# Moving a decoder block's SBUF tiles from multiples of 64 bytes to multiples of 128

## The chip, the cores and the metric

The kernel runs on one NeuronCore of one Trainium2 chip. The metric is the device time of one execution in microseconds, the median of repeated runs. The core has five engines: TensorE (PE, whose weight loads the profile lists apart as PEld), VectorE (DVE), ScalarE (ACT), GpSimd (POOL) and SyncE (SP), which here only issues transfers. The on-chip memory SBUF has 128 partitions; a tile takes the same byte range in all of them, so "address" below means the byte offset within a partition.

## The reference

One decoder block on 512 positions of width 1024, everything in float32, cut to its steps:

```python
h = rms_norm(x, g_mix)
u, q, k, v, gate_logits = split(h @ w_in)
y_pool = causal_multiscale_pool(u, w_pool, pool_scale)      # windows 2, 4, 8, 16
q, k = apply_rope(q), apply_rope(k)
o = diff_attention(q, k, v, lam)       # 4 heads: softmax(q0 k0) - lam * softmax(q1 k1), causal, times v
y_attn = rms_norm(o, g_subln) * (1 - lam_init)
x = x + (concat([y_pool, y_attn]) * sigmoid(gate_logits)) @ w_out
x = x + memory_cross_attention(rms_norm(x, g_cross), rms_norm(mem, g_mem), w_cq, w_ckv, w_co)
x = x + square(relu(rms_norm(x, g_mlp) @ w_up)) @ w_down     # 1024 -> 4096 -> 1024
return rms_norm(x, g_final)
```

The memory `mem` has 256 rows; its product with `w_ckv` gives the keys and the values of the cross attention.

## The kernel before

Activations are kept transposed: 128 features in the partitions, 512 positions along a row. Every operand of a large product is split into a rounded part and a remainder, both float32r (`hi`, `lo`), and `mm3` (L93 to L96) adds three matmuls for each block of 128 features: hi times hi, lo of the streaming operand, lo of the weights.

```python
def mm3(o, lh, ll, rh, rl, start, stop):
    nc.tensor.matmul(o, lh, rh, start=start, stop=False)   # L94
    nc.tensor.matmul(o, lh, rl, start=False, stop=False)   # L95
    nc.tensor.matmul(o, ll, rh, start=False, stop=stop)    # L96
```

The first operand is loaded as weights (a LDWEIGHTS before each matmul), the second streams past them. `tile_mm` makes one output tile of 128x512: eight blocks, so 24 matmuls, with the weights in `whi` and `wlo` and the activations streaming.

The work runs in this order: v (L334 to L338, where `whi`/`wlo` stream and `xg` is loaded); the 20 tiles of `PLAN` (q, k, gate, u), between which a list of due steps (`after`, `tick`) puts the scores, transposes and products of the differential attention and the pooling; the output projection; the memory's keys (`mem_k`, 256 columns wide) and values (`mem_v`); the cross attention's queries with its scores in between (`cross_scores`, 256 columns), and its output; then the MLP in four groups, each of eight up tiles and eight down tiles. The last down tile is cut into two halves of 256 columns so that the final norm can begin early. Weights are fetched three tiles ahead, and VectorE and ScalarE split them two ahead. TensorE's program is in the order in which the code is written; the other engines' is set by a scheduler.

All tiles come from one pool. Each tag (`tmp`, `xg`, `whi`, ...) gets a stretch for its buffers; the stretches follow one another in the order in which the tags are first used, each buffer rounded up to 32 bytes. The first is `vx` (gains and the first block of x), 557 floats or 2228 bytes, which fills 2240. What matters of the result, with the stage in which TensorE reads it:

| tag | what it holds for TensorE | address of the first buffer before, modulo 128 | after, modulo 128 |
|---|---|---|---|
| `cst` (with `ident`) | identity for transposes | 18752, 64 | 18816, 0 |
| `tmp` | squares, pooled rows, softmax rows | 25664, 64 | 25728, 0 |
| `ones` | sums over features | 46720, 0 | 46848, 0 |
| `xg` | normed x; x1 normed; output of the cross attention; activations of the MLP | 61568, 0 | 61696, 0 |
| `whi`, `wlo` | split weights | 94336 and 106624, 0 | 94464 and 106752, 0 |
| `vr` | v | 121152, 64 | 121344, 0 |
| `s` | q, k; normed memory; queries of the cross attention | 137664, 64 | 137856, 0 |
| `at` | transposed softmax rows | 163008, 64 | 163200, 0 |
| `mix` | mixed rows; keys and values of the memory; x2 normed | 185536, 64 | 185728, 0 |

All large buffers are multiples of 1024 bytes long (`xg` and `mix` 4096, `hi` in the first half and `lo` in the second), and the slices that TensorE takes begin at multiples of 512 within them, so a tag's remainder holds for all its reads.

Of the kernel before, what the change touches and what calls it, by code (L numbers as in the profile page):

```python
# [17 lines left out]
P = 128  # L18
T = 512
# [20 lines left out]
NG_COL = LAMS  # L40
# [6 lines left out]
def block_kernel(ctx: ExitStack, tc: tile.TileContext, x0g, xT, memT, wv, wm, wckv, wpool, vecs, csts, outT):  # L47
# [14 lines left out]
    def nm(s):  # L62
        uid[0] += 1
        return f"{s}_{uid[0]}"

    def sb(tag, shape, bufs, dt=F32):
        return pool.tile(shape, dt, tag=tag, name=nm(tag), bufs=bufs)
# [10 lines left out]
    def ps(tag, bufs):  # L78
        return psum.tile([P, T], F32, tag=tag, name=nm(tag), bufs=bufs)
# [20 lines left out]
        S.copy(hi, src)  # L100
        eng.tensor_tensor(lo, src, f(hi), op=ALU.subtract)  # L101

    vx = sb("vx", [P, NG_COL + T], 1)
    vec = vx[:, :NG_COL]
    cst = sb("cst", [P, NCST], 1)
    nc.sync.dma_start(vx, x0g)
# [6 lines left out]
    warm = ps("acc", 2)  # L113
    for j in range(WARM):
        nc.tensor.matmul(warm, idle[:, :P], idle, start=j == 0, stop=j == WARM - 1)
    eps = sb("eps", [P, 16], 1)[:, :1]
    V.memset(eps, EPS)
    one_f = sb("onef", [P, P], 1)
    V.memset(one_f, 1.0)
# [46 lines left out]
    def rsqrt(dst, ssum, scale, v, l, by=None):  # L166

        V.tensor_scalar(v, ssum, scale, EPS, op0=ALU.mult, op1=ALU.add)
        S.activation(l, ssum, AF.Ln, bias=eps, scale=scale)
        S.activation(dst, l, AF.Exp, scale=-0.5)  # L170
        S.activation(l, dst, AF.Square)
        V.scalar_tensor_tensor(l, l, -0.5, v, op0=ALU.mult, op1=ALU.mult)
        if by is not None:
            by(dst)
        V.scalar_tensor_tensor(dst, l, 1.5, dst, op0=ALU.add, op1=ALU.mult)
# [18 lines left out]
    def rstd_rows(sp, n):  # L194
        hi, lo = sp
        o = ps("tr", 2)
        for i in range(n):
            c = slice(i * P, (i + 1) * P)
            nc.tensor.matmul(o[:, 2 * i:2 * i + 2], hi[:, c], ones[:, :2], start=True, stop=False)
            nc.tensor.matmul(o[:, 2 * i:2 * i + 2], lo[:, c], ones[:, :2], start=False, stop=True)  # L200
        r = sb("rrow", [P, 8], 2)[:, :2 * n]
        rsqrt(r, o[:, :2 * n], 1.0 / D, sb("rscr", [P, 8], 4)[:, :2 * n], sb("rscr", [P, 8], 4)[:, :2 * n])
        return r

# [118 lines left out]
    def v_proj():  # L323
# [18 lines left out]
        def stats():  # L342
            r = rstd_full(sp, ss)
            st["rstd"] = r
            rr = rstd_rows(sp, NT)
            V.tensor_tensor(cos_r, cos_r, r, op=ALU.mult)
            V.tensor_tensor(sin_r, sin_r, r, op=ALU.mult)
            vs = []
            for i in range(NT):
                vh = sb("vr", [P, T], 8, F32R)  # L350
                vl = sb("vr", [P, T], 8, F32R)
                scaled(vh, vl, o[i], rr[:, 2 * i:2 * i + 1])
                vs.append((vh, vl))
            st["v"] = vs
            lambdas()
# [190 lines left out]
    def mem_in():  # L546
        mg = {}
        sm = sb("ssm", [P, M], 1)
        for k2 in range(KC // 2):
            t = tmp()  # L550
            nc.sync.dma_start(t, memT[:, 2 * k2:2 * k2 + 2, :])
            pr = pair("s", 6)
            for kk in range(2):
                k = 2 * k2 + kk
                c = slice(kk * M, (kk + 1) * M)
                scaled(pr[:, 0, c], pr[:, 1, c], t[:, c], vec[:, G_MEM + k:G_MEM + k + 1])
                accumulate(sm, k, t[:, c], M)
                mg[k] = (pr[:, 0, c], pr[:, 1, c])
        st["mg"] = mg
        sp = split_sq(sm, M)  # L560

        def stats():
            st["mrstd"] = rstd_full(sp, sm, M)
            st["mrow"] = rstd_rows(sp, MT)

        after(STATM, stats)
# [273 lines left out]
```

## Time and profile before

| | |
|---|---|
| median of 3 runs | 743.44 us (742.29 to 744.35) |
| the profiled execution | 742.82 us, span 741.0 us from its first to its last instruction |
| mean granted TensorE clock | 0.994 |
| TensorE busy | 722.2 us in 3384 matmuls |
| weight loads busy | 598.8 us |
| VectorE, ScalarE, GpSimd busy | 429.4, 354.6, 58.7 us |
| DMA | 78.41 MB, mean 106 GB/s |

The busy time of an engine is that in which at least one of its instructions runs. Matmuls are pipelined: one starts before the last has ended, so their durations add up to more than the busy time, and the distance between two starts is read from the timeline, which lists the instructions by start time (us from the span's start, then the duration).

### The profile page before, as it was taken

What the parts mean: (1) busy time and instruction counts of PE and PEld (TensorE: products, weight loads), DVE (VectorE), ACT (ScalarE), POOL (GpSimd) and SP (SyncE); (2) the same over time, 40 slices, a digit from 0 to 9 for tenths busy, and PEclk for the clock granted to TensorE, in tenths of its full rate; (3) what the DMA queues carried; (4) which work ended last, traced back from release to release, by engine and by line L of the source; (5) the groups of instructions that cost most, each with busy time, mean ns of one, the idle gap of its engine ahead of it and who ended that gap; (6) DMA issues with size and microseconds to landing.
All of it is one profiled execution on the core that took longest, in us unless ns stands there. A gap on an engine that the chain in (4) does not pass through costs nothing.

```text
span 741.0 us, 8888 instructions
## 1 busy us (share of the span) xinstructions
PE 722.2 (97%) x3384; PEld 598.8 (81%) x3384; DVE 429.4 (58%) x677; ACT 354.6 (48%) x589; POOL 58.7 (8%) x50
## 2 busy tenths in 40 slices
PE   8999999999999999999999999999999999999993
PEld 5877888788889888888888888888888888888882
DVE  7597999875987546663665443453434533345336
ACT  7498998676766434343354321342214422234332
POOL 0043112534000000000000000000000000000003
PEclk9999999999999999999999999999999999999997
DMA  8433223142535541210423323223232232232203
GB/s 312 142 113 114 86 73 113 61 162 92 171 114 178 193 140 59 68 47 29 142 85 89 111 86 110 89 86 113 86 99 100 86 113 86 92 107 86 86 0 113
DMA packets 24650, 78.41 MB, mean 106 GB/s; under 512 B 2688, under 2 KB 4736, under 8 KB 24608
## 3 DMA queue, kind: packets, MB, share of 16 engines
q1 hardware_dynamic: 24560, 77.73, 32.3%
q8 instruction: 26, 0.43, 0.3%
q14 instruction: 16, 0.13, 0.1%
q0 software_dynamic: 48, 0.13, 0.0%
HBM read 73.65 MB, written 2.10 MB: 102 GB/s over the span
## 4 chain that ended last, share of the span: by engine, by line
PE 87%; DVE 5%; ACT 4%; DMA 1%; issue 1%; POOL 0%; SPq 0%; DVEq 0%; ACTq 0%
PE acc L94 25%; PE acc L96 24%; PE acc L95 24%; PE sc L94 3%; PE sc L96 3%; PE sc L95 3%; ACT tmp L395 1%; DMA tmp<-xT 1%; DVE mix L734 1%; DVE tmp L393 1%; PE sc L334 1%; ACT tmp L365 1%; PE sc L336 1%; PE sc L338 1%; ACT whi L100 1%
## 5 line engine op out<-in xcount | busy, mean ns | idle before, releaser
L100 ACT CAST whi<-wraw 128x1024 fp32r<-128x1024 f32 (+1 forms) x128 | 133.9, 1047 | 297.1 <-PE acc L95 227.5
L94 PE MATMUL acc<-xg,whi 128*128 128x512 f32 x504 | 198.6, 394 | 0.0
L96 PE MATMUL acc<-xg,wlo 128*128 128x512 f32 x504 | 196.6, 390 | 0.0
L95 PE MATMUL acc<-xg,whi 128*128 128x512 f32 x504 | 196.4, 390 | 0.0
L101 DVE TENSOR_TENSOR wlo<-wraw,whi 128x1024 fp32r<-128x1024 f32 (+1 forms) x128 | 158.3, 1237 | 33.0 <-ACT whi L100 32.6
L94 PE MATMUL acc<-mix,whi 128*128 128x512 f32 x296 | 116.3, 393 | 0.0
L96 PE MATMUL acc<-mix,wlo 128*128 128x512 f32 x296 | 116.2, 392 | 0.0
L95 PE MATMUL acc<-mix,whi 128*128 128x512 f32 x296 | 115.2, 389 | 0.0
L96 PEld LDWEIGHTS acc<-xg,wlo 128*128 128x128 f32 x504 | 94.6, 188 | 20.2
L94 PEld LDWEIGHTS acc<-xg,whi 128*128 128x128 f32 x504 | 94.7, 188 | 19.0
L95 PEld LDWEIGHTS acc<-xg,whi 128*128 128x128 f32 x504 | 94.7, 188 | 18.6
L520 DVE TENSOR_TENSOR vr<-acc,vr 128x512 f32<-128x512 f32 x41 | 28.3, 691 | 109.0 <-PE acc L96 109.0
L745 DVE SCALAR_TENSOR_TENSOR tmp<-acc,rstd 128x512 f32<-128x512 f32 x32 | 22.1, 692 | 84.4 <-PE acc L96 84.3
L96 PEld LDWEIGHTS acc<-mix,wlo 128*128 128x128 f32 x296 | 55.6, 188 | 12.6
L95 PEld LDWEIGHTS acc<-mix,whi 128*128 128x128 f32 x296 | 55.6, 188 | 12.5
L94 PEld LDWEIGHTS acc<-mix,whi 128*128 128x128 f32 x296 | 55.6, 188 | 11.4
L734 POOL TENSOR_TENSOR mix<-mix,tmp 128x256 f32<-128x256 f32 x7 | 6.2, 906 | 547.9 <-ACT mix L716 546.6
L101 DVE TENSOR_TENSOR xg<-tmp,xg 128x512 fp32r<-128x512 f32 x32 | 22.1, 692 | 0.3 <-ACT xg L100 0.3
L395 ACT ACTIVATE tmp<-tmp,small 128x128 f32<-128x128 f32 (+3 forms) x32 | 17.9, 560 | 5.8 <-DVE small L393 5.6
L100 ACT CAST xg<-tmp 128x512 fp32r<-128x512 f32 x32 | 19.8, 620 | 1.0
L746 ACT ACTIVATE tmp<-tmp 128x512 f32<-128x512 f32 x32 | 20.1, 632 | 0.0
L211 DVE TENSOR_TENSOR ss<-ss,tmp 128x512 f32<-128x512 f32 x27 | 18.6, 688 | 1.6 <-ACT tmp L210 1.4
(229 smaller groups left out, 944.9 us busy)
## 6 DMA issues: line engine op xcount, KB each, us to landing
wraw<-wm SPq DMA_DIRECT2D x108, 512.0 KB, 3.3
wraw<-wckv SPq DMA_DIRECT2D x16, 512.0 KB, 3.8
s<-s SPq DMA_DIRECT2D x8, 256.0 KB, 3.6
vr<-xT SPq DMA_DIRECT2D x8, 256.0 KB, 5.0
outT<-mix SPq DMA_DIRECT2D x8, 256.0 KB, 2.2
tmp<-xT SPq DMA_DIRECT2D x7, 256.0 KB, 6.8
wraw<-wv SPq DMA_DIRECT2D x3, 512.0 KB, 6.6
tmp<-memT SPq DMA_DIRECT2D x4, 256.0 KB, 4.7
```

Of the source, the lines that this page charges most:

```text
L94: nc.tensor.matmul(o, lh, rh, start=start, stop=False)
L95: nc.tensor.matmul(o, lh, rl, start=False, stop=False)
L96: nc.tensor.matmul(o, ll, rh, start=False, stop=stop)
L100: S.copy(hi, src)
L101: eng.tensor_tensor(lo, src, f(hi), op=ALU.subtract)
L211: V.tensor_tensor(ss, ss, sq, op=ALU.add)
L334: nc.tensor.matmul(o[i], xg[k][0][:, tb], wh[:, c], start=k == 0, stop=False)
L395: S.activation(e[:, :n], e[:, :n], AF.Exp, bias=mn, scale=-1.0, accum_out=sm[:, c:c + 1])
L520: V.tensor_tensor(t, o, t, op=ALU.add)
L734: eng.tensor_tensor(y3[j][:, i, c], y3[j][:, i, c], r, op=ALU.mult)
L745: V.scalar_tensor_tensor(t, o, 0.0, st["r2"], op0=ALU.max, op1=ALU.mult)
L746: S.activation(t, t, AF.Square)
```

## The change

Three small tiles are allocated longer, and used at their old length. `vx` becomes 576 floats (2304 bytes), `eps` goes from 64 to 128 bytes, the two buffers of `rrow` (row scales) from 32 to 64 bytes each. So the tags after them move: by 64 bytes from `cst` on, by 128 from `onef` on, by 192 from `rscr` on. Nothing else is changed: all engines run the same instructions in the same order.

```diff
-    vx = sb("vx", [P, NG_COL + T], 1)
+    vx = sb("vx", [P, NG_COL + T + 19], 1)[:, :NG_COL + T]
     vec = vx[:, :NG_COL]
...
-    eps = sb("eps", [P, 16], 1)[:, :1]
+    eps = sb("eps", [P, 32], 1)[:, :1]
...
-        r = sb("rrow", [P, 8], 2)[:, :2 * n]
+        r = sb("rrow", [P, 16], 2)[:, :2 * n]
```

## The prediction

> **What bounds the kernel now.** I read the page first (busy time, the clock row, the chain that ended last), then TensorE's waits, then its groups, and last the start times of single matmuls in the timeline.
>
> ```profile
> span 741.0 us, 8888 instructions
> ...
> PE 722.2 (97%) x3384; PEld 598.8 (81%) x3384; DVE 429.4 (58%) x677; ACT 354.6 (48%) x589; POOL 58.7 (8%) x50
> ...
> PEclk9999999999999999999999999999999999999997
> ...
> PE 87%; DVE 5%; ACT 4%; DMA 1%; issue 1%; POOL 0%; SPq 0%; DVEq 0%; ACTq 0%
> ```
>
> TensorE is busy for 97% of the span at a granted clock of 0.9 or more in every slice but the last, and it is 87% of the chain that ended last. Its list of waits begins like this and only gets shorter:
>
> ```profile
> PE sc L391 <- DMA s<-s: 1.6, 1, 1.6
> PE acc L115 <- DVE tmp L112: 1.2, 1, 1.2
> ```
>
> So what sets the time is the distance from one matmul's start to the next, and a change that issues the same instructions can gain or lose only there, or by making some operand late. The change touches addresses alone. The groups give no hint that an address matters (the last number before the second bar is the mean in ns):
>
> ```profile
> L94 PE MATMUL acc<-xg,whi 128*128 128x512 f32 x504 | 198.6, 394 | 0.0
> L94 PE MATMUL acc<-mix,whi 128*128 128x512 f32 x296 | 116.3, 393 | 0.0
> L94 PEld LDWEIGHTS acc<-xg,whi 128*128 128x128 f32 x504 | 94.7, 188 | 19.0
> L94 PEld LDWEIGHTS acc<-mix,whi 128*128 128x128 f32 x296 | 55.6, 188 | 11.4
> ```
>
> A tile `xg` that begins on a multiple of 128 bytes and a tile `mix` that begins 64 bytes past one have the same duration. But 394 ns is a pipelined matmul's length, and matmuls overlap; 3384 of them would not fit otherwise. What counts is the pitch, start to start. In a row `mix,whi` the first name is the operand that streams, the second the one that is loaded as weights. Rows of the timeline, at the borders of output tiles of the MLP (24 matmuls of 512 columns each); the first number is the start in us:
>
> ```profile
> 463.94 0.40 PE L94 MATMUL acc<-mix,whi 128*128 128x512 f32 x1
> 469.45 0.39 PE L94 MATMUL acc<-mix,whi 128*128 128x512 f32 x1
> ...
> 507.90 0.40 PE L94 MATMUL acc<-xg,whi 128*128 128x512 f32 x1
> ...
> 513.39 0.39 PE L94 MATMUL acc<-xg,whi 128*128 128x512 f32 x1
> ...
> 551.47 0.40 PE L94 MATMUL acc<-mix,whi 128*128 128x512 f32 x1
> ```
>
> Up, reading `mix`: from 469.45 to 507.90 lie seven tiles, 168 matmuls: 38.45/168 = 228.9 ns. Down, reading `xg`: 513.39 to 551.47, again 168: 38.08/168 = 226.7 ns. The first tile of each half is slower (5.51 and 5.49 us against 5.49 and 5.44). That is the one place where the trace shows a price for the 64 bytes: 2.2 ns per matmul. It is a confounded comparison, since `mix` also lies elsewhere in the memory.
>
> **The change, term by term.** The five engines' instructions and their order are the same; every tile after `vx` moves by 64 to 192 bytes. Before, `xg`, `whi`, `wlo`, `ones` lie on multiples of 128 and `cst`, `tmp`, `vr`, `s`, `at`, `mix` 64 bytes off; after, all lie on one. The pairs fall into five groups.
>
> A. `mix` streams, `whi`/`wlo` loaded. If it then runs like `xg`, a group of up matmuls takes what a down group takes: 551.47 - 507.90 = 43.57 instead of 507.90 - 463.94 = 43.96 us, 0.39 less, and there are 4 groups: 1.56 us. The output projection also streams `mix`, 8 tiles of 24; three of its tiles:
>
> ```profile
> 188.26 0.39 PE L94 MATMUL acc<-mix,whi 128*128 128x512 f32 x1
> ...
> 204.74 0.39 PE L94 MATMUL acc<-mix,whi 128*128 128x512 f32 x1
> ```
>
> 16.48/72 = 228.9 ns, the same as in the MLP, so 192 x 2.2 ns = 0.43 us. Together -2.0 us. Lower end -2.2 (all 960 at 226.7, and no slow first tile); upper end +4.2 (all at the 233.3 ns of the next term).
>
> B and C. The memory's values and keys. Keys stream `s` (64 off, 256 columns), values load `s` as weights (64 off, 512 columns streamed from `whi`):
>
> ```profile
> 216.42 0.28 PE L94 MATMUL acc<-s,whi 128*128 128x256 f32 x1
> ...
> 221.75 0.28 PE L96 MATMUL acc<-s,wlo 128*128 128x256 f32 x1
> ...
> 225.47 0.28 PE L94 MATMUL acc<-s,whi 128*128 128x256 f32 x1
> ...
> 239.60 0.40 PE L94 MATMUL sc<-whi,s 128*128 128x512 f32 x1
> ...
> 262.00 0.39 PE L94 MATMUL sc<-xg,whi 128*128 128x512 f32 x1
> ```
>
> Values: (262.00 - 239.60)/96 = 233.3 ns, the slowest pitch at 512 columns. At 226.7 they save 0.63 us; some of it may stay, as in the first tiles above, so B is -0.5 (0 to -0.6). Keys: 47 steps from 216.42 to 221.75 are 113.4 ns each (half of 226.7, nothing to gain), the 120 from 225.47 to 239.60 take 117.8. One place has 256 columns with both operands on multiples of 128, the first half of the last tile:
>
> ```profile
> 721.10 0.28 PE L94 MATMUL sc<-xg,whi 128*128 128x256 f32 x1
> ...
> 723.97 0.28 PE L94 MATMUL sc<-xg,whi 128*128 128x256 f32 x1
> ```
>
> 2.87/24 = 119.6 ns. So at 256 columns the aligned pair is slower than the misaligned. If the keys go there, 48 matmuls lose 6.2 ns and 144 lose 1.8: C is +0.6 us (from -0.6, all at 113.4, to +0.6). I take the end of the row that has the alignment the keys will have.
>
> D. Scores of the cross attention, `mix` and `s`, both 64 off, 256 columns, 4 heads of 24:
>
> ```profile
> 276.29 0.28 PE L94 MATMUL sc<-mix,s 128*128 128x256 f32 x1
> ...
> 279.16 0.40 PE L94 MATMUL acc<-xg,whi 128*128 128x512 f32 x1
> ```
>
> 2.87/24 = 119.6 ns, what the aligned pair takes too: 0 (down to -0.6 at 113.4). That equal offsets behave alike, whether 0 or 64, speaks for the relation of the two streams as the cause, and not for the line on which one begins.
>
> E. The attention phase and the small sums. Between scores, transposes and sums, q, k, gate and u tiles run in pieces of nine or so:
>
> ```profile
> 120.46 0.47 PE L94 MATMUL acc<-xg,whi 128*128 128x512 f32 x1
> ...
> 122.63 0.22 PE L390 MATMUL sc<-s,s 128*128 128x128 f32 x1
> ```
>
> 2.17 us for nine, where 226.7 ns would make 2.04. Of the 0.13 too much, 0.08 stands in the first one's length (0.47 against 0.39), which is the change of shape and stays; 0.05 is a slow pitch after the interruption. Some 30 such pieces make 1.5 us, and the interrupting matmuls themselves, about 150, are at most the 6.6 ns of term B too slow, 0.5 to 1 us. Whether an aligned interruption disturbs less is not to be seen: a down group's first tile loses the same 0.05 us (5.49 - 5.44) with aligned operands, though after a misaligned predecessor. I take -0.5 (0 to -2).
>
> The rest costs nothing by its rows. Vector work on a `vr` tile (64 off) lasts as long as on `xg` tiles:
>
> ```profile
> L520 DVE TENSOR_TENSOR vr<-acc,vr 128x512 f32<-128x512 f32 x41 | 28.3, 691 | 109.0 <-PE acc L96 109.0
> L101 DVE TENSOR_TENSOR xg<-tmp,xg 128x512 fp32r<-128x512 f32 x32 | 22.1, 692 | 0.3 <-ACT xg L100 0.3
> ```
>
> and it idled 109 us for TensorE there, so it also has cover. No transfer changes in size; the largest wait of TensorE on one is the 1.6 us above. `eps` and `rrow` are read at their first columns only, as before.
>
> Sum: -2.0 - 0.5 + 0.6 + 0 - 0.5 = -2.4 us. The profiled execution took 742.82 us (1.8 around its span) and becomes 740.4; it stands 0.6 below the median of 743.44, so against the median 741.0.
>
> **Rivals.** No change: the address does not matter, and `mix` is slow because it streams x2g and the mixed rows, or lies in another part of the memory. For it: equal durations in the groups, and every slow tile also has a high address (`s`, `mix`). Against it: `xg` is fast in the output of the cross attention and in the down half alike, so the stage is not what matters. 743.4. The Trainium skill (SBUF — State Buffer, section Specifications) gives a line of 16 bytes as the unit of full-rate access, and in its section Who interferes with whom says that TensorE never waits on anyone; both homes begin on such a line, so by it this rival holds and the sum is 0. The trace has 228.9 against 226.7 ns, which that page would have to explain otherwise.
>
> Slower: the relation between the two streams matters over a longer period than 128 bytes. Today `xg` and `whi` have the same offset modulo 256 and `mix` is 64 bytes from `whi`; afterwards `mix` is 128 bytes from `whi` modulo 256, a distance that no long run of the trace has. If those 960 matmuls then pay what the values pay, 233.3 instead of 228.9, that is +4.2, and C adds 0.6: 748.2. It decides from a pitch of about 231 ns on. The only rows near it, `at` with `vr` in the attention, are 12 matmuls that never settle.
>
> Everything settles: A, B, C and D at their low ends and E at -1.5: -2.2 - 0.6 - 0.6 - 0.6 - 1.5 = -5.5, so 737.9. For it: the keys' first 48 matmuls hold 113.4. Against it: 119.6 with both aligned.
>
> **How the numbers follow.** The sum's case 0.52, no change 0.24, everything settles 0.14, slower 0.10. A difference under 0.3% (2.2 us) is about what these runs can't tell from none. The sum's case lies just beyond it, so 0.32 of its 0.52 count as faster, with the 0.14 of full settling 0.46; 0.20 and the 0.24 of no change make 0.44 within; 0.10 slower. The range leaves out the slower case and the outer part of full settling (it ends at a gain of 4.8), and reaches 1 us above the median for no change: 738.6 to 744.4. The sum's case alone would be 739.8 to 742.2.
>
> **What would show it.** A right: 226.7 ns per matmul in the up halves, tiles of 5.44 us; wrong: still 228.9, or over 231. B: the values' 96 matmuls in 21.8 us instead of 22.4. C: 119.6 ns on all keys; at 113.4 the time comes out 1.2 us lower. E: less than 2.17 us for a piece of nine. The prediction fails at large if the up halves keep their pitch, since A is most of it, or if `xg` tiles, whose offset to `whi` stays, change theirs.

## The result: 0.6% slower

The changed kernel takes 747.72 us (median of 6 runs, 746.54 to 749.11) against 743.1 (6 runs, 742.29 to 744.35). The ratio is 1.0061, 95% interval 1.0046 to 1.0075. The forecast was 741.0, with 738.6 to 744.4 as its range.

The profiled execution took 746.97 us. Its page, in the lines that answer to those of before:

```profile
span 745.1 us, 8888 instructions
...
PE 726.2 (97%) x3384; PEld 599.4 (80%) x3384; DVE 429.7 (58%) x677; ACT 354.5 (48%) x589; POOL 58.8 (8%) x50
...
PEclk9999999999999999999999999999999999999997
...
L94 PE MATMUL acc<-xg,whi 128*128 128x512 f32 x504 | 198.6, 394 | 0.0
...
L94 PE MATMUL acc<-mix,whi 128*128 128x512 f32 x296 | 117.0, 395 | 0.0
```

The span grew by 4.1 us and TensorE's busy time by 4.0, at the same clock (0.994); the weight loads grew by 0.6, and no other engine's busy time moved by more than 0.3. Its list of waits begins with 1.5 us, as before with 1.6. So the loss is in the distance between the matmuls themselves. The groups show it only as a hint: `mix` went from 393 to 395 ns, `xg` kept its 394. The timeline at the same borders of output tiles as before (start in us first):

```profile
465.57 0.40 PE L94 MATMUL acc<-mix,whi 128*128 128x512 f32 x1
471.16 0.40 PE L94 MATMUL acc<-mix,whi 128*128 128x512 f32 x1
...
510.36 0.39 PE L94 MATMUL acc<-xg,whi 128*128 128x512 f32 x1
...
515.82 0.39 PE L94 MATMUL acc<-xg,whi 128*128 128x512 f32 x1
...
553.89 0.40 PE L94 MATMUL acc<-mix,whi 128*128 128x512 f32 x1
```

Up, on `mix`: (510.36 - 471.16)/168 = 233.3 ns per matmul, where it was 228.9. Down, on `xg`: (553.89 - 515.82)/168 = 226.6, as before. An up group takes 44.79 us instead of 43.96; four groups make +3.3. In the output projection three tiles take (205.25 - 188.45)/72 = 233.3 ns per matmul instead of 228.9, which is +0.8 on its 192:

```profile
188.45 0.40 PE L94 MATMUL acc<-mix,whi 128*128 128x512 f32 x1
...
205.25 0.40 PE L94 MATMUL acc<-mix,whi 128*128 128x512 f32 x1
```

These two are +4.1 us, the whole growth of the span. The keys and values of the memory:

```profile
217.09 0.28 PE L94 MATMUL acc<-s,whi 128*128 128x256 f32 x1
...
222.66 0.28 PE L96 MATMUL acc<-s,wlo 128*128 128x256 f32 x1
...
226.27 0.28 PE L94 MATMUL acc<-s,whi 128*128 128x256 f32 x1
...
240.52 0.39 PE L94 MATMUL sc<-whi,s 128*128 128x512 f32 x1
...
262.82 0.39 PE L94 MATMUL sc<-xg,whi 128*128 128x512 f32 x1
```

Keys: 118.5 ns in the first 47 steps (113.4 before), 14.25/120 = 118.8 after (117.8 before), +0.4 us in all. Values: 22.30/96 = 232.3 ns (233.3 before), -0.1 us. The small remainder, the other way, lies in the rest of the program.

### The profile page after: what moved, and what is told of

Same layout as the page of the kernel before. It is cut to its first block, busy times and chain, and to the rows that moved or that the text cites. A ratio compares the mean times of both kernels' runs of the same rounds, so it can differ in the third digit from the quotient of the medians.

```text
span 745.1 us, 8888 instructions
## 1 busy us (share of the span) xinstructions
PE 726.2 (97%) x3384; PEld 599.4 (80%) x3384; DVE 429.7 (58%) x677; ACT 354.5 (48%) x589; POOL 58.8 (8%) x50
## 4 chain that ended last, share of the span: by engine, by line
PE 88%; DVE 5%; ACT 4%; DMA 1%; issue 1%; POOL 0%; SPq 0%; DVEq 0%; ACTq 0%
PE acc L94 25%; PE acc L96 24%; PE acc L95 24%; PE sc L96 3%; PE sc L94 3%; PE sc L95 3%; ACT tmp L395 1%; DVE mix L734 1%; DMA tmp<-xT 1%; DVE tmp L393 1%; PE sc L334 1%; ACT tmp L365 1%; PE sc L336 1%; PE sc L338 1%; ACT whi L100 1%
## 5 line engine op out<-in xcount | busy, mean ns | idle before, releaser
L94 PE MATMUL acc<-mix,whi 128*128 128x512 f32 x296 | 117.0, 395 | 0.0
L95 PE MATMUL acc<-mix,whi 128*128 128x512 f32 x296 | 116.9, 395 | 0.0
```

## The experiments

Theory R is the prediction's slower rival: what counts is the distance between the tile that streams and the tile that is loaded as weights, modulo 256 bytes (the streaming tile's address minus the weight tile's; the two directions differ, as the table below shows). P and A are its rivals: `mix` is slow for its place far up in the memory (P), or for its own remainder (A). Times are compared with the kernel before on the same chip, 742.8 us in both sets.

**`mix` alone, one step further.** From the changed kernel, a gap ahead of `mix`:

```diff
+        if not mixed:
+            sb("gap", [P, 32], 1)
         pr = pair("mix", 8)
```

> The changed kernel, with mix alone moved on by 128 bytes, so that it lies 256 bytes from whi and wlo modulo 512 (0 modulo 256) and still on a multiple of 128. Theory R (what counts is the distance between the streaming tile and the weight tile, modulo 256): the up halves and the output projection fall from 233.3 ns per matmul to 226.7, 960 x 6.6 = 6.3 us less than the changed kernel, about 741.4. Theory P (mix is slow because it lies far up in the memory): the pitch stays at 233.3 and the time at 747.7. Theory A (what counts is the streaming tile's own remainder, 384 modulo 512 in the changed kernel): remainder 0 is one that no fast tile has had, so the pitch is open, but xg has been fast at 128 and 256. If the distance counts modulo 512, the pitch may be anything from 226.7 to 240.

It took 740.36 us, with a ratio to the kernel before of 0.997 (0.9959 to 0.9981). That is 7.4 us less than the changed kernel's median, which was timed in another set, and 6.6 by the spans of the profiled executions (738.5 against 745.1). The second to the eighth up tile lie between these rows, 38.08/168 = 226.7 ns:

```profile
468.40 0.39 PE L94 MATMUL acc<-mix,whi 128*128 128x512 f32 x1
...
506.48 0.39 PE L94 MATMUL acc<-xg,whi 128*128 128x512 f32 x1
```

`mix` is as fast as `xg` there, 128 bytes further up, so P is out. And 256 is as good as 0: what counts repeats after 256 bytes, not after 512.

**The dose: `xg` at the bad distance as well.**

```diff
+        if not ready and i == 0:
+            sb("gapw", [P, 32], 1)
         hi = sb("whi", [P, D], 3, F32R)
```

> The changed kernel with 128 bytes put between xg and whi: xg keeps its address, and whi, wlo and everything behind move on by 128. The distance of mix to whi stays 128, that of xg becomes 384 modulo 512 (128 modulo 256). Theory R: now the xg tiles pay as well, the down halves and q, k, g, u go from 226.7 to about 233.3: 1600 x 6.6 = 10.5 us more than the changed kernel, less the slow first matmuls that they have already, 756 to 758. Theories P and A: xg has not moved, so the down halves stay at 226.7 and the time at 747.7.

It took 753.33 us, ratio 1.0138 (1.0116 to 1.016): 5.6 us more than the changed kernel (6.4 by the spans, 751.5 against 745.1), less than R had named. In the down half:

```profile
519.78 0.39 PE L94 MATMUL acc<-xg,whi 128*128 128x512 f32 x1
...
558.82 0.39 PE L94 MATMUL acc<-mix,whi 128*128 128x512 f32 x1
```

39.04/168 = 232.4 ns instead of 226.6, though `xg` did not move: what streams is not slow in itself, it is slow against these weights, and A is out with it. Nor are the weights slow for their own address: in the fifth experiment below `whi` lies at 94592 as it does here, and the down halves run at 226.7 ns.

R's size was too large, for three reasons. It took 233.3 ns, and `xg` settles at 232.4 (0.9 ns less on some 1600 matmuls, 1.4 us). The 480 matmuls of q, k, g and u, whose steps average 234.1 ns with the interruptions, went only to 236.7. And `mix`, whose distance to `whi` is the same as in the changed kernel, became faster, from 233.3 to 232.4 (0.8 us on its 960), which theory R does not explain:

```profile
475.17 0.40 PE L94 MATMUL acc<-mix,whi 128*128 128x512 f32 x1
...
514.21 0.40 PE L94 MATMUL acc<-xg,whi 128*128 128x512 f32 x1
```

39.04/168 = 232.4. So one distance can settle at two pitches. The keys of the kernel before had shown the same, 113.4 ns in the first 47 steps and 117.8 later, with the same two tiles. What decides between them was not tested: the distance fixes the pitch to about 1 ns at 512 columns and to about 4 at 256.

**The part alone.** From the kernel before, `mix` on by 64 bytes: it then begins on a multiple of 128, and all tiles ahead of it lie where they did.

```diff
+        if not mixed:
+            sb("gap", [P, 16], 1)
         pr = pair("mix", 8)
```

> The kernel before with mix alone moved on by 64 bytes, so that it begins on a multiple of 128 and lies 128 bytes from whi; every tile ahead of it stays where it was. Theory R: 233.3 ns in the up halves and the output projection, 960 x 4.4 = 4.2 us more than before, 747.3 (the keys, which were the other loss of the change, do not move). The prediction's reading (a multiple of 128 is what helps): 226.7 and 741. Theory P: 743.

It took 747.77 us, ratio 1.0065 (1.0048 to 1.0081): the loss of the whole change. From 471.33 to 510.53 its seven up tiles take the 39.20 us of the changed kernel:

```profile
471.33 0.40 PE L94 MATMUL acc<-mix,whi 128*128 128x512 f32 x1
...
510.53 0.39 PE L94 MATMUL acc<-xg,whi 128*128 128x512 f32 x1
```

**The distances measured by themselves.** A kernel of nothing but matmuls, executed once, with weight tiles `wa` to `wq` 32 bytes apart modulo 512:

```python
for n in (T, M):
    for t in w:
        run(mov, t, n)              # 48 matmuls
    for k in (0, 2, 4, 6, 8, 10):
        o = run(nov, w[k], n)
```

> Leaves the block out and only runs matmuls of float32r operands: one streaming tile (mov at 128 modulo 512) against 17 weight tiles wa to wq that lie 32 bytes apart modulo 512, so that the distance falls from 384 by 32 with each letter (wm has 0, wi 128, we 256, wa 384), 48 matmuls each, first 512 columns wide and then 256; after each sweep a second streaming tile (nov at 192) against wa, wc, we, wg, wi, wk. Theory R: the pitch at 512 columns repeats every 8 letters, with 226.7 ns at wm and we, 233.3 at wi, wq and wa, 229 at wk; nov gives the same at the same distance (233.3 with wg, 226.7 with wk's neighbour in distance). Theory A: all letters are equal for mov, and differ from nov. At 256 columns R expects 120 at wm and less at a distance of 64 (wk, wc). Distances that are not multiples of 64 have not occurred yet: if the unit is 64 bytes, they go with a neighbour.

The timeline merges each 48; the pitch is the difference of two starts over 48.

```profile
52.01 11.05 PE L121 MATMUL acc<-mov,we 128*128 128x512 f32 x48
62.89 11.35 PE L121 MATMUL acc<-mov,wf 128*128 128x512 f32 x48
74.08 11.36 PE L121 MATMUL acc<-mov,wg 128*128 128x512 f32 x48
85.28 11.40 PE L121 MATMUL acc<-mov,wh 128*128 128x512 f32 x48
96.52 11.32 PE L121 MATMUL acc<-mov,wi 128*128 128x512 f32 x48
107.68 11.37 PE L121 MATMUL acc<-mov,wj 128*128 128x512 f32 x48
118.88 11.16 PE L121 MATMUL acc<-mov,wk 128*128 128x512 f32 x48
129.88 11.36 PE L121 MATMUL acc<-mov,wl 128*128 128x512 f32 x48
141.07 11.05 PE L121 MATMUL acc<-mov,wm 128*128 128x512 f32 x48
151.96 11.35 PE L121 MATMUL acc<-mov,wn 128*128 128x512 f32 x48
163.15 11.36 PE L121 MATMUL acc<-mov,wo 128*128 128x512 f32 x48
...
219.10 11.16 PE L121 MATMUL acc<-nov,we 128*128 128x512 f32 x48
230.09 11.06 PE L121 MATMUL acc<-nov,wg 128*128 128x512 f32 x48
240.99 11.36 PE L121 MATMUL acc<-nov,wi 128*128 128x512 f32 x48
252.19 11.32 PE L121 MATMUL acc<-nov,wk 128*128 128x512 f32 x48
263.35 5.86 PE L121 MATMUL acc<-mov,wa 128*128 128x256 f32 x48
```

| distance, bytes | weights, with `mov` | ns per matmul |
|---|---|---|
| 0 | `wm` | 226.9 |
| 32 | `wl` | 233.1 |
| 64 | `wk` | 229.2 |
| 96 | `wj` | 233.3 |
| 128 | `wi` | 232.5 |
| 160 | `wh` | 234.2 |
| 192 | `wg` | 233.3 |
| 224 | `wn` | 233.1 |
| 256 | `we` | 226.7 |

`nov`, 64 bytes off in itself, gives 229.0 with `we` (320, that is 64), 227.1 with `wg` (256, that is 0) and 232.5 with `wk` (128): the same by distance, another by address. The expectation's 233.3 for `nov` with `wg` was a slip: their distance is 256. So the pitch follows the distance, and of the multiples of 32 only those of 256 are fast, with 64 in second place. The direction counts: 64 gives 229.2 ns, 192 (that is -64) gives 233.3. The kernel before had `mix` at that second-best distance, 64, and the change took it to 128.

At 256 columns the order is another, and 0 is among the slowest.

```profile
303.18 5.79 PE L121 MATMUL acc<-mov,wh 128*128 128x256 f32 x48
308.81 5.85 PE L121 MATMUL acc<-mov,wi 128*128 128x256 f32 x48
314.50 5.91 PE L121 MATMUL acc<-mov,wj 128*128 128x256 f32 x48
...
331.57 5.91 PE L121 MATMUL acc<-mov,wm 128*128 128x256 f32 x48
337.31 5.84 PE L121 MATMUL acc<-mov,wn 128*128 128x256 f32 x48
```

The steps are 117.3 ns at 160, 118.5 at 128 and 119.6 at 0; at 64 they are 117.7, less than at 0, as expected. It is the 119.6 that the prediction had read from the last tile.

**Everything at distance 0.** From the kernel before, four pads that bring all of TensorE's tiles to 128 modulo 256:

```diff
-    vx = sb("vx", [P, NG_COL + T], 1)
+    vx = sb("vx", [P, NG_COL + T + 19], 1)[:, :NG_COL + T]
-    eps = sb("eps", [P, 16], 1)[:, :1]
+    eps = sb("eps", [P, 64], 1)[:, :1]
-        r = sb("rrow", [P, 8], 2)[:, :2 * n]
+        r = sb("rrow", [P, 16], 2)[:, :2 * n]
-        gsub = sb("gsub", [P, 16], 1)[:, :1]
+        gsub = sb("gsub", [P, 48], 1)[:, :1]
```

> The kernel before with pads at vx, eps, rrow and gsub, so that cst, tmp, ones, xg, whi, wlo, vr, s, at and mix all lie at 128 modulo 256, that is at distance 0 from each other modulo 256. Theory R with the table just measured (0: 226.7 ns at 512 columns, 120 at 256): mix 960 x -2.2 = -2.1 us against before, the values 96 x -6.6 = -0.6, the keys 192 x +3 = +0.6, small stages -0.3: about 740.4, no more than 0.5 us from the version that moved mix alone. A rival by which every pair has a distance of its own would leave more or less than that.

It took 739.56 us, ratio 0.9957 (0.9945 to 0.997), faster than both kernels. The values now take (260.57 - 238.78)/96 = 227.0 ns, the keys (238.78 - 224.38)/120 = 120.0:

```profile
224.38 0.28 PE L94 MATMUL acc<-s,whi 128*128 128x256 f32 x1
...
238.78 0.40 PE L94 MATMUL sc<-whi,s 128*128 128x512 f32 x1
...
260.57 0.39 PE L94 MATMUL sc<-xg,whi 128*128 128x512 f32 x1
```

**The same distances, every tile 64 bytes off.** This version has `NG_COL + T + 35` in `vx` and is otherwise the last one. No tile that TensorE reads begins on a multiple of 128.

> The last version with 64 bytes more in vx: every tile that TensorE reads now begins 64 bytes past a multiple of 128, and all distances are still 0 modulo 256. Theory R: the same time as the last version within 0.1%, about 740.4, pitch 226.7 in up and down halves. If a multiple of 128 is worth anything in itself, as the change supposes and the prediction's sum took over, it is slower: with 228.9 ns on all 2600 matmuls of 512 columns by 5.7 us.

It took 739.96 us, ratio 0.9959 (0.9947 to 0.9971): this is the last one's time, and the intervals are all but the same. A multiple of 128 is worth nothing in itself.

**Finer distances, narrower weights, bfloat16.** Again a kernel of nothing but matmuls, executed once.

> Leaves the block out and only runs matmuls, 48 of a kind, 512 columns, one weight tile wgt. First mov at distances of 0, 4, 8, 16, 32, 64, 128 and 256 bytes (banks pa to ph in this order), then weights of 64 and of 32 columns at distances 0, 64, 128 (pa, pf, pg), then bfloat16 operands at 0, 32, 64, 128, 256 bytes (pa, pe to ph), last the first pair again (pb). Theory L (the two streams of TensorE, weights and moving operand, get into each other's way while a weight load overlaps a matmul): with fewer columns of weights the penalty at 128 shrinks or goes, and 226.7 itself may fall; rival M (the penalty lies in the moving operand's own reading): it stays with 32 columns. Below 32 bytes no value is known: if a read covers 64 bytes, 4 to 16 go with 0 or with their neighbour 32 (233.3). With bfloat16 I expect near 216, as the last two of the warm-up, and a smaller effect or none, since half the bytes are read.

```profile
18.53 11.52 PE L122 MATMUL pb<-mov,wgt 128*128 128x512 f32 x48
29.89 11.35 PE L122 MATMUL pc<-mov,wgt 128*128 128x512 f32 x48
...
96.47 11.20 PE L122 MATMUL pa<-mov,wgt 128*64 128x512 f32 x48
107.51 11.16 PE L122 MATMUL pf<-mov,wgt 128*64 128x512 f32 x48
118.51 11.17 PE L122 MATMUL pg<-mov,wgt 128*64 128x512 f32 x48
129.52 11.27 PE L122 MATMUL pa<-mov,wgt 128*32 128x512 f32 x48
140.62 11.29 PE L122 MATMUL pf<-mov,wgt 128*32 128x512 f32 x48
151.75 11.23 PE L122 MATMUL pg<-mov,wgt 128*32 128x512 f32 x48
162.82 10.53 PE L122 MATMUL pa<-bmov,bwgt 128*128 128x512 bf16 x47
...
193.91 10.52 PE L122 MATMUL pg<-bmov,bwgt 128*128 128x512 bf16 x47
204.27 10.52 PE L122 MATMUL ph<-bmov,bwgt 128*128 128x512 bf16 x47
```

Four bytes are the worst distance measured, 236.7 ns; 8 and 16 give 233.1 and 231.7. With 64 columns of weights the distances 0, 64 and 128 are already nearly alike, 230.0, 229.2 and 229.4 ns, and with 32 columns they are again, 231.3, 231.9 and 230.6. That the distance stops mattering fits L, in which the overlapping weight load is one side of it; that the pitch then stays at 229 to 232, above the 226.7 that 128 columns reach at distance 0, fits neither L nor M. With bfloat16 the distances 0 to 128 give 215.8 to 216.0 ((193.91 - 162.82)/144 is 215.9 for the first three, 10.36/48 is 215.8 from `pg` to `ph`), and the steps within `ph`, at 256, are 216; one record of each 48 is missing from the trace.

That the pitch goes by the distance modulo 256, with float32r operands and 128 columns of weights, is shown, to within the 1 ns named above at 512 columns. By what mechanism the two operands hinder each other is left open.

## Why the prediction was wrong

- What bounds the kernel held: the difference is in TensorE's pitch, and none of its waits grew by more than 0.5 us.
- Term A failed, at the step "If it then runs like `xg`". It priced the 64 bytes as a property of `mix` and put -2.0 us; the runs show a property of the pair, and +4.1. Its upper end, +4.2 at the values' 233.3 ns, is where it landed. The range of the text did not take that end in, since it hung on the slower rival, which had a chance of 0.10. That rival named what counts, the place (128 modulo 256) and the time: 748.2, measured 747.72. That its time fits so well is in part luck. Its 233.3 ns came from the values, whose distance was 192, and at 128 the matmuls alone give 232.5.
- The clue was in the prediction itself. Term D noted that two tiles 64 bytes off behave like two on a multiple of 128, and that this speaks for the relation of the streams. Term A did not follow it: by relation, `xg` with `whi` is a row for distance 0, and no settled row existed for 128. The pooling's product, which streams `tmp` (64 modulo 256) past `s` (192), was a second row at 128, which the rival did not name beside `at` with `vr`: 12 matmuls in threes, 231.8 ns on average to the next start, already above the 231 from which the rival decides. An unknown distance should have had its two ends, 226.7 and 233.3, at even chances.
- B: -0.5 forecast, -0.1 measured, for the same reason: the values' distance became 128, not 0. With distance 0 they do reach 227.0.
- C: +0.6 forecast, +0.4 measured. The sign was right for another reason; 118.5 to 118.8 ns is the pitch at a distance of 128, and the 119.6 of the last tile is that of 0.
- D: 0, as forecast; that distance did not change modulo 256. E: -0.5 forecast and nothing to be seen of it (the stretch from the end of v to the output projection took 143.2 us before and 143.3 after); the tiles of the attention phase run against `whi` at distance 0 before and after.
- The rival of no change is refuted by the result. The Trainium skill (TensorE: Matmul & The Clock Gate, section Step-by-step: what each phase is for) says: "Loading the next tile's weights doesn't steal SBUF read bandwidth from the running matmul." With float32r, 226.9 against 233.3 ns by distance alone is not what that sentence leads one to expect, though no run here shows that read bandwidth is the cause. With bfloat16 nothing here speaks against it, and the 215.8 is what the Trainium skill (the same page, section Back-to-back issue gap) gives for an isolated matmul of 512 columns (N / 2.4 + 2.5 ns). The 131 ns that this section gives for a sustained stream at 512 columns is not what the run shows.

## What to carry to other kernels

Where TensorE is busy back to back with float32r operands, the pitch in the timeline, start to start over whole tiles, is the number to watch, since durations in the groups hide up to 3%. For matmuls of 512 columns with 128 columns of weights, place the streaming tile and the weight tile a multiple of 256 bytes apart rather than aligning either; four pads were worth 0.4% here. At 256 columns that distance is not the best one. Before an alignment is changed, list for each pair the distance before and after: a change that is uniform in remainders need not be uniform in distances.

## What had not been expected of the hardware

The pitch of float32r matmuls depends on where TensorE's two operands lie relative to each other: 226.9 ns at 0 modulo 256, 229.2 at 64, 232.5 to 234.2 at the other multiples of 32, 236.7 at 4 bytes, for 512 columns. It does not depend on this alone: one distance, 128, settled at 233.3 ns for `mix` in the changed kernel and at 232.4 in the second experiment. At 256 columns the equal remainder is not the best but among the worst, 119.6 ns against 117.3 at 160. With 64 or 32 weight columns instead of 128 the matmuls were slower than the best case with 128: at distance 0, 230.0 and 231.3 ns against 226.9.
